# S5 matrices E built in their final layout from factors read with broadcast; q·B for eight groups at a time; adaLN pieces summed in one PSUM bank

## The chip, the core and the metric

The kernel runs on one core of a Trainium2 chip. Its metric is the time of one execution on the device, in microseconds (us), as the median of several runs. The core has five engines with a queue each, in which instructions run in order: TensorE (PE, with weight loads shown as PEld), VectorE (DVE), ScalarE (ACT), GpSimd (POOL) and SyncE (SP, which only issues transfers). They wait for each other through semaphores. Transfers issued by SP, ACT and POOL share 16 DMA engines.

## The reference, cut to what matters

One inference step of a two-layer backbone for 128 context tokens and 256 latent tokens (384 columns), width 1024. Each layer is a half-weighted SwiGLU, a mixer, a half-weighted SwiGLU; every sub-layer is modulated by adaLN vectors and followed by a layer norm. The mixer of layer 0 is a bidirectional S5 state-space layer:

```
x <- LayerNorm(ALPHA * x + w * gate * sublayer(x * (1 + scale) + shift))
(shift, scale, gate) = SiLU(cond) @ ada_w + ada_b            # per layer and sub-layer

abar = exp(dt * a)                                           # complex, per direction, group (64), state (64)
q    = (abar - 1) / a
bb   = q * b                                                 # complex, b: (group, state, 16)
s[t] = abar * s[t-1] + bb @ u[t]                             # forward, and backward in t
y    = Re(c @ s) + d_skip * u
```

The kernel runs the scan in blocks of eight tokens. For that it makes, from the parameters alone, three tables: E (what eight inputs add to a block's state: bb times powers of abar, one 128x128 matrix for each group and for the real and imaginary part), G (what a state gives to eight outputs: c times powers of abar) and the taps (the products of bb and G, for outputs from inputs inside a block).

## The kernel before, in words

Six sub-layers run one after the other: `ffn(0)`, `s5(1)`, `ffn(2)`, `ffn(3)`, `lru(4)`, `ffn(5)`. A float32 product is made of three TensorE products of rounded parts (`mm3`, lines 264 to 266): each weight tile of 1024 columns is fetched by SP into one of seven buffers `raw`, ACT makes `hi` from it (line 253) and DVE the rest `lo` (line 256); a step of `mm3` takes `hi` twice and `lo` once. I call the three matmuls of one `mm3` a step.

`ffn(0)` has 22 up-projection tiles, in splits of 8, 7 and 7, each split followed by a down loop over the eight output tiles m: up 0 (16 steps of `mm3` for each f), down 0 (64 steps), up 1 (112), down 1 (56), up 2 (112), down 2 (56). After every second k of an up tile, and three times in each m of down 0 and down 1, it calls `side()` from `beside(125, 42, 9)`. That is a slot, 124 up to the end of up 2. A slot either does one `ada_fill` (line 144: four matmuls of one half piece of `ada_w`, two trace instructions each; 42 of them, spread over 125 slots) or one step of the generator `s5_tables`. What is left of the generator at the end of up 2 is run through in `gen_done`, ahead of down 2. The order on PE is as written in the program; that of the other engines in `ffn(0)` is made by the scheduler, with the generator's instructions put some way ahead of their place (`high_priority`).

The generator first works out powers and q on DVE (steps up to line 684). Then, for each of 16 chunks `ch` of four groups, in five steps: `store_e` turns the four groups' E, eight PE transposes (line 731), two ACT copies into `s5eo` (732), and a store from the POOL queue to `etd` (734); `build_e(ch + 1)` loads 128 KB of b and c, negates c_re on DVE into `ncr` (692), makes bb by six DVE products and sums of 128x64 (lines 645 to 650, called through `cmul`), and E by six of 128x512; `taps` makes 16 small matmuls from bb and G (742), two ACT copies and two DVE additions, and a store to `kd`; `build_g(ch + 1)` makes the real part of G on DVE (716 to 718, 128x640) and the imaginary part on POOL (720 to 722), and stores it to `gd` from the POOL queue. E has one buffer, G two. `ada_w` loads go through the POOL queue too (line 127).

`ada_fill` sums the two halves of a piece in one PSUM bank; ACT copies the first piece of a group (151), DVE adds each further piece (153); `ada_flush` turns the sum with two matmuls (193).

`s5(1)` reads E, the taps and G back from memory. In its outputs part six more half pieces of `ada_w` run on PE between the products of tiles m (`ADAS = 4, 2`, after m = 2 and m = 3).

Of the kernel before, what the change touches and what calls it, by code (L numbers as in the profile page):

```python
# [23 lines left out]
Q = 8  # L24
# [10 lines left out]
ADAS = 4, 2  # L35
# [10 lines left out]
def backbone(ctx, tc, a, o):  # L46
# [60 lines left out]
    ada_acc = [None, None, 0]  # L107
# [22 lines left out]
    def ada_fill(n=1, load=True, bank=psaux, flush=True):  # L130


        for _ in range(n):
# [4 lines left out]
            if kh == 0:  # L138
                if flush:
                    ada_flush(bank)  # L140
                ada_acc[0] = bank()
            acc = ada_acc[0]
            for q in range(4):
                PE.matmul(acc[32 * q:32 * q + 32, :256], cond[:, kh * 4 + q, 6 - 2 * j:38 - 2 * j], w[:, q, :],  # L144
                          start=kh == 0, stop=kh == 1, tile_position=(0, 32 * q))
            if load:
                ada_load()
            if kh == 1:
                if j == 0:
# [4 lines left out]
                if j == len(group) - 1:  # L154
                    ada_pend.append((l, s, group, ada_acc[1]))
# [400 lines left out]
    kd = dram.tile([2048, 240], F32, name="kd")  # L556
    td = dram.tile([128, 64, 128], F32, name="td")
# [26 lines left out]
    def s5_tables(gp_):  # L584
# [49 lines left out]
        pw = gp_.tile([128, 2, 9, 64], F32, name="s5pw", tag="gch", bufs=2)  # L634
# [41 lines left out]
        pe = gp_.tile([128, 2, 8, 64], F32, name="s5pe")  # L676
# [10 lines left out]
        def build_e(ch):  # L687
            g0 = ch * 4
            bc = gp_.tile([128, 4, 64], F32, name="s5bc", tag="bc", bufs=2)
            nc.sync.dma_start(bc, a["s5bc"][ch])  # L690
            ncr = gp_.tile([128, 64], F32, name="s5ncr", tag="ncr")
            V.tensor_scalar(ncr, bc[:, 2, :], -1.0, None, op0=OP.mult)
            bb = gp_.tile([128, 2, 80], F32, name="s5bb", tag="bb", bufs=2)
            G.memset(bb[:, :, 64:80], 0.0)

            qv = lambda t: vw(t, g0, [[1, 4], [0, 16]])
            bv = lambda ri: vw(bc, ri * 64, [[16, 4], [1, 16]])
            ov = lambda ri: vw(bb, ri * 80, [[16, 4], [1, 16]])
            cmul(ov(0), ov(1), qv(sn), qv(cs), bv(0), bv(1), [[16, 4], [1, 16]])

            E = gp_.tile([128, 4, 2, 128], F32, name="s5E", tag="ech")
            pv = lambda ri: vw(pe, ri * 512 + g0, [[1, 4], [64, 8], [0, 16]])
            bv = lambda ri: vw(bb, ri * 80, [[16, 4], [0, 8], [1, 16]])
            ov = lambda ri: vw(E, ri * 128, [[256, 4], [16, 8], [1, 16]])
            cmul(ov(0), ov(1), pv(0), pv(1), bv(0), bv(1), [[128, 4], [16, 8], [1, 16]])
            return bc, ncr, bb, E

        def build_g(ch, bc, ncr):

            g0 = ch * 4  # L710
# [15 lines left out]
        def store_e(ch, E):  # L726
            eo = gp_.tile([128, 1024], F32, name="s5eo", tag="eo")
            for j in range(2):
                pt = psum()
                for b in range(4):  # L730
                    PE.transpose(pt[:, b * 128:b * 128 + 128], E[:, j * 2 + b // 2, b % 2, :], ident)
# [22 lines left out]
        for _ in range(9):  # L754
            yield
# [670 lines left out]
```

## Time and profile before

| | us |
|---|---|
| median of 3 runs | 1634.89 (1634.05 to 1637.48) |
| profiled execution, its own time | 1631.38 |
| span in that profile, first to last instruction | 1629.6 |
| PE busy, DVE busy, ACT busy, POOL busy | 1546.1, 1278.5, 709.4, 336.5 |
| mean granted TensorE clock, as a share of full | 0.974 |

All times further down are of that one profiled execution, counted from the span's start. A matmul's busy time is modelled and matmuls overlap, so two that follow each other start closer together than either lasts; the starts in the timeline tell PE's pace. Likewise a DVE instruction's record begins a little before the one ahead of it ends. The name in front of the arrow is the tile that is written.

### The profile page before, as it was taken

How to read it: one execution, taken by the hardware profiler on the slowest of the kernel's cores; microseconds unless marked ns; L12 is line 12 of the kernel's file. 1: busy time of each engine (PE TensorE's matmuls, PEld its weight loads, DVE VectorE, ACT ScalarE, POOL GpSimd, SP SyncE). 2: the span in 40 equal slices, each digit the busy share in tenths (PEclk: the TensorE clock that was granted, in tenths of full speed). 3: DMA queues.
4: the chain of work that ended last, by engine and by line, in shares of the span. 5: the costliest groups of instructions: out<-in, count | busy, mean ns of one | idle time of the engine just before them, and what ended most of it. 6: DMA issues, size and time to landing. Idle time of an engine off the chain costs nothing.

```text
span 1629.6 us, 25853 instructions
## 1 busy us (share of the span) xinstructions
PE 1546.1 (95%) x9554; PEld 1474.6 (90%) x9554; DVE 1278.5 (78%) x2750; ACT 709.4 (44%) x1157; POOL 336.5 (21%) x524
## 2 busy tenths in 40 slices
PE   7989999999988999999999999999989599999996
PEld 5877887889988999999999999999978599999995
DVE  4999999977796569979777998977797889644445
ACT  4423332335655366333345632334569366323332
POOL 0155445423380013000002300000165322000001
PEclk9989999999999999999999999999999799999997
DMA  9766776877878533667556356755513243544321
GB/s 352 260 215 224 232 244 237 259 244 275 129 272 257 201 133 118 230 202 243 173 171 208 117 188 214 243 193 160 193 64 118 76 157 123 160 153 139 100 77 39
DMA packets 108543, 301.19 MB, mean 185 GB/s; under 512 B 28384, under 2 KB 40160, under 8 KB 108160
## 3 DMA queue, kind: packets, MB, share of 16 engines
q1 hardware_dynamic: 85792, 249.62, 46.3%
q0 software_dynamic: 13152, 46.70, 8.7%
q10 hardware_dynamic: 9472, 3.21, 1.4%
q8 instruction: 75, 1.23, 0.3%
q14 instruction: 52, 0.43, 0.1%
HBM read 275.89 MB, written 27.80 MB: 186 GB/s over the span
## 4 chain that ended last, share of the span: by engine, by line
PE 70%; DVE 20%; DMA 3%; issue 3%; ACT 3%; POOL 1%; SPq 0%; ACTq 0%; DVEq 0%; POOLq 0%
PE mm L264 22%; PE mm L266 22%; PE mm L265 22%; DVE lo L256 2%; DVE hl L317 1%; PE aux L144 1%; DMA adaw<-in_ada_w 1%; DVE s5sb L881 1%; DVE w L878 1%; DVE w L460 1%; ACT w L322 1%; DVE lxc L1090 1%; PE mm L917 1%; DVE s5sb L880 1%; DVE w L879 1%
## 5 line engine op out<-in xcount | busy, mean ns | idle before, releaser
L264 PE MATMUL mm<-hh,hi 128*128 128x384 f32 (+1 forms) x1568 | 542.1, 346 | 14.5 <-DVE hh L1143 7.3
L265 PE MATMUL mm<-hl,hi 128*128 128x384 f32 (+1 forms) x1568 | 535.7, 342 | 10.2 <-DVE hl L317 10.1
L266 PE MATMUL mm<-hh,lo 128*128 128x384 f32 (+1 forms) x1568 | 535.4, 341 | 5.0 <-DVE lo L256 5.0
L253 ACT ACTIVATE hi<-raw 128x1024 fp32r<-128x1024 f32 (+1 forms) x332 | 323.2, 976 | 495.7 <-PE mm L265 467.1
L256 DVE TENSOR_TENSOR lo<-raw,hi 128x1024 fp32r<-128x1024 f32 (+1 forms) x344 | 393.6, 1148 | 164.4 <-ACT hi L253 154.1
L264 PEld LDWEIGHTS mm<-hh,hi 128*128 128x128 f32 x1568 | 298.7, 191 | 32.9 <-issue 15.7
L265 PEld LDWEIGHTS mm<-hl,hi 128*128 128x128 f32 x1568 | 299.0, 191 | 13.3 <-DVE hl L317 12.7
L266 PEld LDWEIGHTS mm<-hh,lo 128*128 128x128 f32 x1568 | 298.6, 190 | 7.0 <-DVE lo L256 7.0
L264 PE MATMUL mm<-zh,hi 128*128 128x384 f32 x704 | 240.5, 342 | 2.0 <-ACT zh L479 2.0
L265 PE MATMUL mm<-zl,hi 128*128 128x384 f32 x704 | 237.5, 337 | 1.8 <-DVE zl L480 1.6
L266 PE MATMUL mm<-zh,lo 128*128 128x384 f32 x704 | 237.0, 337 | 0.0
L264 PEld LDWEIGHTS mm<-zh,hi 128*128 128x128 f32 x704 | 132.9, 189 | 9.6 <-issue 6.3
L179 DVE SCALAR_TENSOR_TENSOR dump<-raw,cb 128x512 bf16<-128x512 f32 x160 | 109.9, 687 | 39.7 <-DMA raw<-in_ada_t 39.2
L265 PEld LDWEIGHTS mm<-zl,hi 128*128 128x128 f32 x704 | 133.1, 189 | 2.6 <-DVE zl L480 2.6
L266 PEld LDWEIGHTS mm<-zh,lo 128*128 128x128 f32 x704 | 133.2, 189 | 0.0
L479 ACT ACTIVATE zh<-w 128x384 fp32r<-128x384 f32 x88 | 46.1, 525 | 160.5 <-DVE w L487 154.1
L179 DVE SCALAR_TENSOR_TENSOR raw<-raw,cb 128x512 f32<-128x512 f32 x160 | 110.1, 688 | 2.6
L395 POOL TENSOR_TENSOR t<-mv 128x3 f32<-128x3 f32 x5 | 4.0, 799 | 446.0 <-ACT mv L394 446.0
L264 PE MATMUL mm<-ph,hi 128*128 128x388 f32 x224 | 77.4, 346 | 0.0
L265 PE MATMUL mm<-pl,hi 128*128 128x388 f32 x224 | 76.6, 342 | 0.0
L266 PE MATMUL mm<-ph,lo 128*128 128x388 f32 x224 | 76.3, 341 | 0.0
L545 DVE SCALAR_TENSOR_TENSOR r<-mm,gate,r 128x128 f32<-128x128 f32 (+1 forms) x144 | 53.2, 410 | 20.5 <-PE mm L266 20.5
(356 smaller groups left out, 1983.1 us busy)
## 6 DMA issues: line engine op xcount, KB each, us to landing
raw<-in_up SPq DMA_DIRECT2D x176, 512.0 KB, 4.4
raw<-in_ada_t SPq DMA_DIRECT2D x80, 512.0 KB, 4.2
raw<-in_down SPq DMA_DIRECT2D x56, 512.0 KB, 3.9
adaw<-in_ada_w POOLq DMA_DIRECT2D x42, 512.0 KB, 5.3
adaw<-in_ada_w SPq DMA_DIRECT2D x22, 512.0 KB, 7.9
raw<-in_down SPq DMA_DIRECT2D x48, 192.0 KB, 2.4
gd<-s5G POOLq DMA_DIRECT2D x16, 512.0 KB, 4.8
etd<-s5eo POOLq DMA_DIRECT2D x16, 512.0 KB, 5.5
```

The lines of the kernel that those rows point to most:

```text
L144: PE.matmul(acc[32 * q:32 * q + 32, :256], cond[:, kh * 4 + q, 6 - 2 * j:38 - 2 * j], w[:, q, :], start=kh == 0, stop=kh == 1, tile_positi ...
L179: V.scalar_tensor_tensor(out, wq, 1.0, cb[:, g, q * 512:q * 512 + 512], op0=OP.mult, op1=OP.mult, accum_out=part[:, t, g, q:q + 1])
L253: S.activation(hi[:, :n], raw[:, :n], AF.Copy)
L256: V.tensor_tensor(lo[:, :n], raw[:, :n], hi[:, :n], op=OP.subtract)
L264: PE.matmul(ps, hi[:, c:c + 128], xh, start=start, stop=False)
L265: PE.matmul(ps, hi[:, c:c + 128], xl, start=False, stop=False)
L266: PE.matmul(ps, lo[:, c:c + 128], xh, start=False, stop=stop)
L317: V.tensor_tensor(hl[:, k, :n], src, hh[:, k, :n], op=OP.subtract)
L322: S.activation(h[:, c0:c1], r[:, k, c0:c1], AF.Identity, bias=bs[:, k, g:g + 1], scale=gs[:, k, g:g + 1])
L460: V.scalar_tensor_tensor(t[:, c0:c1], self.ms[:, c0:c1], gw[:, g:g + 1], t[:, c0:c1], op0=OP.mult, op1=OP.add)
L479: S.activation(zh, z, AF.Copy)
L545: V.scalar_tensor_tensor(r[:, m, c0:c1], ps[:, c0:c1], gate[:, m, g:g + 1], r[:, m, c0:c1], op0=OP.mult, op1=OP.add)
```

## The change

In the generator:

- E is no longer built by state rows and turned. The factors are turned once: `pq` (q times the powers, six DVE instructions of 128x512) goes through eight PE transposes and is stored to a memory tensor `ptd`. For each chunk SP then reads `pt` (512 KB, every row of `ptd` to 16 partitions) and `bt` (256 KB, b in a new host layout, to eight groups of partitions), one chunk ahead and into two buffers each; six DVE instructions of 128x512 make E from them in the layout in which it is stored, and the store to `etd` goes out of E itself from the POOL queue. E keeps one buffer (tag `ech`, shared with the tables `pe` and `rows`).
- bb is made for eight groups (two chunks) at once, six DVE instructions of 128x128. `ncr` is made on POOL. b and c are loaded for two chunks at a time. G (tag `gch`) has one buffer instead of two.
- A chunk takes four steps of the generator instead of five.

In the adaLN pieces: all half pieces of a group are summed in one PSUM bank, which is copied once by ACT; DVE adds only where a group is closed early. `beside(125, 42, 9)` becomes `beside(125, 40, 9)` and `ADAS` becomes `4, 4`: two half pieces move from `ffn(0)` to `s5(1)`, where a load of `ada_w` follows the first four.

```
-ADAS = 4, 2
+ADAS = 4, 4
...
+            begin = acc is None
+            if begin:
+                acc = ada_acc[0] = bank()
+            done = kh == 1 and j == len(group) - 1
+            end = done or close and x == n - 1
             for q in range(4):
                 PE.matmul(acc[32 * q:32 * q + 32, :256], cond[:, kh * 4 + q, 6 - 2 * j:38 - 2 * j], w[:, q, :],
-                          start=kh == 0, stop=kh == 1, tile_position=(0, 32 * q))
+                          start=begin, stop=end, tile_position=(0, 32 * q))
...
-            if kh == 1:
-                if j == 0:
+            if end:
+                if ada_acc[1] is None:
...
-        pw = gp_.tile([128, 2, 9, 64], F32, name="s5pw", tag="gch", bufs=2)
+        pw = gp_.tile([128, 2, 9, 64], F32, name="s5pw", tag="gch")
...
+        def scaled(b):
...
+            cmul(ov(0), ov(1), qv(sn), qv(cs), bv(0), bv(1), [[16, 8], [1, 16]])
...
-            G.tensor_tensor(ov(1), cv(ncr, 0), pv(1), op=OP.mult)
-            G.tensor_tensor(p, cv(bc, 3), pv(0), op=OP.mult)
+            ncr = z
+            G.tensor_scalar(ncr, two["s5c"][ch // 2][:, 0, ch % 2 * 64:ch % 2 * 64 + 64], -1.0, None, op0=OP.mult)
+            G.tensor_tensor(ov(1), vw(ncr, 0, [[16, 4], [0, 10], [1, 16]]), pv(1), op=OP.mult)
+            G.tensor_tensor(p, cv(1), pv(0), op=OP.mult)
...
-                for b in range(4):
-                    PE.transpose(pt[:, b * 128:b * 128 + 128], E[:, j * 2 + b // 2, b % 2, :], ident)
-                S.activation(eo[:, j * 512:j * 512 + 512], pt, AF.Copy)
-                yield
-            nc.gpsimd.dma_start(etd[ch], eo)
...
+        cmul(pv(pq, 0), pv(pq, 1), pv(pe, 0), pv(pe, 1), qv(sn), qv(cs), [[64, 8], [1, 64]])
+        scaled(0)
+        Gt = build_g(0)
+        for _ in range(10):
+            yield
...
+        def load_e(ch):
+
+            pt = gp_.tile([128, 1024], F32, name="s5pt", tag="pt", bufs=2)
+            nc.sync.dma_start(pt, bass.AP(ptd.tensor, ptd.offset + ch * 1024, [[16384, 8], [0, 16], [1, 1024]]))
+            bt = gp_.tile([128, 512], F32, name="s5bt", tag="bt", bufs=2)
+            nc.sync.dma_start(bt, bass.AP(a["s5bt"].tensor, a["s5bt"].offset + ch * 8192, [[0, 8], [512, 16], [1, 512]]))
+            return pt, bt
+
+        def build_e(ch, pt, bt):
+
+            E = gp_.tile([128, 4, 2, 128], F32, name="s5E", tag="ech")
...
+            cmul(pv(E, 0), pv(E, 1), pv(pt, 0), pv(pt, 1), bv(0), bv(1), [[128, 4], [64, 2], [1, 64]])
+            nc.gpsimd.dma_start(etd[ch], E.rearrange("p g r c -> p (g r c)"))
...
         for ch in range(16):
-            yield from store_e(ch, cur[3])
-            nxt = build_e(ch + 1) if ch < 15 else None
+            taps(ch, two["bb"], Gt)
             yield
-            taps(ch, cur[2], Gt)
+            if ch < 15:
+                fac.append(load_e(ch + 1))
+            if ch % 2 and ch < 15:
+                scaled(ch // 2 + 1)
             yield
-            if nxt:
-                Gt = build_g(ch + 1, *nxt[:2])
-            cur = nxt
+            build_e(ch, *fac[ch])
+            yield
+            if ch < 15:
+                Gt = build_g(ch + 1)
...
-                        ada_load(6, nc.sync)
+                        ada_load(7, nc.sync)
...
-                                    ada_fill(ADAS[m - 2], False, psum, False)
+                                    ada_fill(ADAS[m - 2], False, psum, False, True)
+                                    if m == 2:
+                                        ada_load(4, nc.sync)
...
-        norm = ffn(0, (8, 7, 7), None, beside(125, 42, 9), gen_done, first)
+        norm = ffn(0, (8, 7, 7), None, beside(125, 40, 9), gen_done, first)
```

How this stands in the engines' queues: on PE, before, the end of up 2 holds the last E's eight transposes and the last taps (`mm<-s5G,s5bb`), directly ahead of down 2, whose first step is the one with `zh`:

```order
L266 MATMUL mm<-hh,lo 128x384
L731 MATMUL mm<-ident,s5E 128x128 x8
L742 MATMUL mm<-s5G,s5bb 32x128 x16
L144 MATMUL aux<-adaw,cond 32x256 x4
L264 MATMUL mm<-zh,hi 128x384
```

In the changed kernel (its line numbers are 6 to 34 higher; 270 to 272 are the three of a step) the last taps stand in the middle of up 2:

```order
L272 MATMUL mm<-hh,lo 128x384
L776 MATMUL mm<-s5G,s5bb 32x128 x16
L270 MATMUL mm<-hh,hi 128x384
L271 MATMUL mm<-hl,hi 128x384
L272 MATMUL mm<-hh,lo 128x384
```

No transposes stand there any more, and behind the last taps there are still 64 steps and six half pieces to the end of up 2.

On DVE, before, part of one chunk in up 1, from the end of a G to the first products of the next E (`s5bb` is bb, `s5tp` holds products):

```order
L718 TENSOR_TENSOR s5G<-s5tp 128x4x160
L645 TENSOR_TENSOR s5tp<-s5t_209,s5bc 128x64
L748 TENSOR_TENSOR s5ks<-s5ks,mm 128x16
L646 TENSOR_TENSOR s5tp<-s5t_210,s5bc 128x64
L749 SCALAR_TENSOR_TENSOR s5ks<-s5mask,s5dsk,s5ks 128x16
L647 TENSOR_TENSOR s5bb<-s5tp 128x64
L692 TENSOR_SCALAR s5ncr<-s5bc 128x64
L648 TENSOR_TENSOR s5tp<-s5t_209,s5bc 128x64
L649 TENSOR_TENSOR s5tp<-s5t_210,s5bc 128x64
L650 TENSOR_TENSOR s5bb<-s5tp 128x64
L645 TENSOR_TENSOR s5tp<-s5pe,s5bb 128x512
L646 TENSOR_TENSOR s5tp<-s5pe,s5bb 128x512
```

In the changed kernel, a chunk in up 1 without a new bb, from G to the end of E (`s5pt`, `s5bt` are the broadcast factors):

```order
L722 TENSOR_TENSOR s5G<-s5tp 128x4x160
L262 TENSOR_TENSOR lo<-raw,hi 128x1024
L652 TENSOR_TENSOR s5tp<-s5pt,s5bt 128x512
L653 TENSOR_TENSOR s5tp<-s5pt,s5bt 128x512
L782 TENSOR_TENSOR s5ks<-s5ks,mm 128x16
L654 TENSOR_TENSOR s5E<-s5tp 128x4x128
L783 SCALAR_TENSOR_TENSOR s5ks<-s5mask,s5dsk,s5ks 128x16
L655 TENSOR_TENSOR s5tp<-s5pt,s5bt 128x512
L656 TENSOR_TENSOR s5tp<-s5pt,s5bt 128x512
L657 TENSOR_TENSOR s5E<-s5tp 128x4x128
```

The six instructions of E have kept their size; those of bb are gone from this chunk and stand, twice as wide, in the next. Counted up to the last G write, DVE's queue holds 41 `lo` after the start of the power table instead of 51, and 12 evacuations of an up tile instead of 17.

## Rows read from the trace of the kernel before

**Rows 1.** The page's first part: busy us (share of the span), instructions.

```profile
PE 1546.1 (95%) x9554; PEld 1474.6 (90%) x9554; DVE 1278.5 (78%) x2750; ACT 709.4 (44%) x1157; POOL 336.5 (21%) x524
```

**Rows 2.** Windows: busy of PE, PEld, DVE, ACT, POOL; clock, DMA share, GB/s.

```profile
109.00:164.00 55.00, 49.86 (x398) 42.02 (x397) 54.19 (x89) 16.01 (x27) 28.83 (x30) 0.91 0.63 206
164.00:240.00 76.00, 76.00 (x597) 68.18 (x599) 73.31 (x118) 25.79 (x44) 34.40 (x40) 1.00 0.75 237
240.00:284.00 44.00, 39.98 (x342) 32.29 (x343) 42.70 (x71) 13.39 (x22) 21.87 (x25) 0.99 0.73 251
284.00:358.00 74.00, 74.00 (x606) 66.11 (x604) 65.58 (x111) 25.50 (x44) 28.79 (x36) 0.98 0.75 244
...
68.00:354.00 286.00, 274.88 (x2108) 239.62 (x2115) 275.28 (x475) 90.69 (x148) 129.10 (x146) 0.97 0.70 230
```

**Rows 3.** Timeline of PE in up 0: start us, us, what, count.

```profile
103.45 0.60 PE L731 MATMUL mm<-ident,s5E 128*128 128x128 f32 x4
...
104.07 0.34 PE L265 MATMUL mm<-hl,hi 128*128 128x384 f32 x1
104.24 0.34 PE L266 MATMUL mm<-hh,lo 128*128 128x384 f32 x1
```

**Rows 4.** Groups by line on PE, 68 to 354: count | busy, mean ns | idle before.

```profile
L144 PE MATMUL aux<-adaw,cond 128*32 128x256 f32 x304 | 25.2, 404 | 0.0
L731 PE MATMUL mm<-ident,s5E 128*128 128x128 f32 x120 | 20.3, 289 | 5.5 <-DVE s5E L650 4.7 <-DVE s5E L647 0.8
```

**Rows 5.** Single lines, whole trace: ns min/median/max, first and last start us.

```profile
L718 DVE TENSOR_TENSOR s5G<-s5tp x16: 812/824/1961, 97.4 to 353.5; 128x640 f32<-128x640 f32 x16
...
L731 PE MATMUL mm<-ident,s5E x128: 270/272/421, 103.4 to 357.3; 128*128 128x128 f32 x128
```

**Rows 6.** Groups by line and shape on DVE, 68 to 354.

```profile
L647 DVE TENSOR_TENSOR s5E<-s5tp 128x512 f32<-128x512 f32 x16 | 13.5, 844 | 4.0 <-PE mm L731 3.6
...
L153 DVE TENSOR_TENSOR adae<-adae,aux 128x256 f32<-128x256 f32 x15 | 6.2, 411 | 1.1 <-PE aux L144 1.1
...
L692 DVE TENSOR_SCALAR s5ncr<-s5bc 128x64 f32<-128x64 f32 x15 | 5.3, 356 | 0.4 <-DMA s5bc<-in_s5bc 0.4
...
L645 DVE TENSOR_TENSOR s5tp<-s5pw 128x128 f32<-128x128 f32 x1 | 0.3, 283 | 0.0
```

**Rows 7.** Timeline of DVE in down 0: start us, us, what.

```profile
132.50 1.21 DVE L256 TENSOR_TENSOR lo<-raw,hi 128x1024 fp32r<-128x1024 f32 x1
133.63 0.22 DVE L645 TENSOR_TENSOR s5tp<-s5t,s5bc 128x64 f32<-128x64 f32 x1
133.77 0.21 DVE L646 TENSOR_TENSOR s5tp<-s5t,s5bc 128x64 f32<-128x64 f32 x1
...
134.93 0.69 DVE L645 TENSOR_TENSOR s5tp<-s5pe,s5bb 128x512 f32<-128x512 f32 x1
135.54 2.06 DVE L646 TENSOR_TENSOR s5tp<-s5pe,s5bb 128x512 f32<-128x512 f32 x1
```

**Rows 8.** Timeline of POOL at the same place.

```profile
135.38 1.67 POOL L722 TENSOR_TENSOR s5G<-s5G,s5tq 128x640 f32<-128x640 f32 x1
```

**Rows 9.** Groups by line on POOL, 68 to 354.

```profile
L722 POOL TENSOR_TENSOR s5G<-s5G,s5tq 128x640 f32<-128x640 f32 x16 | 28.5, 1780 | 0.7
L720 POOL TENSOR_TENSOR s5G<-s5ncr,s5pg 128x640 f32<-128x640 f32 x16 | 25.2, 1576 | 6.0 <-PE mm L742 4.3 <-DVE s5pg L682 1.6
L721 POOL TENSOR_TENSOR s5tq<-s5bc,s5pg 128x640 f32<-128x640 f32 x16 | 24.3, 1518 | 5.4 <-DVE s5pg L682 4.2 <-DMA s5bc<-in_s5bc 0.4
...
L531 POOL TENSOR_SCALAR gate<-mod 128x16 f32<-128x16 f32 x1 | 0.4, 393 | 0.2 <-DVE s5ncr L692 0.2
```

**Rows 10.** DMA issues, 40 to 340: KB each, median us to landing.

```profile
etd<-s5eo POOLq DMA_DIRECT2D x14, 512.0 KB, 5.5
```

**Rows 11.** Timeline of PE in the outputs part of s5(1), with idle before.

```profile
502.03 6.87 PE L917 MATMUL mm<-al,raw 128*128 128x98 f32 x32 [3.94 <-DVE al L893]
...
522.30 3.78 PE L917 MATMUL aux<-al,raw 128*128 128x98 f32 x32 [1.29 <-ACT s5Y L921]
```

More of the change, by code (lines that the diff above doesn't have):

```diff
@@ L106, in backbone @@
     ada_done = set()
-    ada_acc = [None, None, 0]
+    ada_acc = [None, None]
     ada_pend = []
@@ L128, in ada_load, with ada_fill @@
             ada_loaded.append((c, w, extra))
-    def ada_fill(n=1, load=True, bank=psaux, flush=True):
-        for _ in range(n):
+    def ada_fill(n=1, load=True, bank=psaux, flush=True, close=False):
+        for x in range(n):
             if not ada_loaded:
@@ L153, in ada_fill @@
                     V.tensor_tensor(ada_acc[1], ada_acc[1], acc[:, :256], op=OP.add)
-                if j == len(group) - 1:
-                    ada_pend.append((l, s, group, ada_acc[1]))
+                ada_acc[0] = None
+            if done:
+                ada_pend.append((l, s, group, ada_acc[1]))
+                ada_acc[1] = None
     def vec_pool():
@@ L708, in build_g, with load2 @@
-        def build_g(ch, bc, ncr):
-            g0 = ch * 4
-            Gt = gp_.tile([128, 4, 2, 160], F32, name="s5G", tag="gch", bufs=2)
+        two = {"s5b": [], "s5c": []}
+        def load2(n, b):
+            two[n].append(gp_.tile([128, 2, 128], F32, name=n, tag=n, bufs=2))
+            nc.sync.dma_start(two[n][b], a[n][b])
+        def scaled(b):
+            bt = two["s5b"][b]
+            bb = gp_.tile([128, 2, 144], F32, name="s5bb", tag="bb")
+            G.memset(bb[:, :, 128:144], 0.0)
+            qv = lambda t: vw(t, b * 8, [[1, 8], [0, 16]])
+            bv = lambda ri: vw(bt, ri * 128, [[16, 8], [1, 16]])
+            ov = lambda ri: vw(bb, ri * 144, [[16, 8], [1, 16]])
+            cmul(ov(0), ov(1), qv(sn), qv(cs), bv(0), bv(1), [[16, 8], [1, 16]])
+            two["bb"] = bb
@@ L724, in build_g @@
             return Gt
[L726 to L729, printed above, removed]
[L730 to L734 removed]
+        for b in range(2):
+            load2("s5b", b)
+            load2("s5c", b)
+        pq = gp_.tile([128, 2, 8, 64], F32, name="s5pq", tag="pt", bufs=2)
+        pv = lambda t, ri: vw(t, ri * 512, [[64, 8], [1, 64]])
+        qv = lambda t: vw(t, 0, [[0, 8], [1, 64]])
+        cmul(pv(pq, 0), pv(pq, 1), pv(pe, 0), pv(pe, 1), qv(sn), qv(cs), [[64, 8], [1, 64]])
[3 more added lines that the diff above has]
+            yield
+        rows = gp_.tile([128, 2, 4, 128], F32, name="s5rows", tag="ech")
+        for ri in range(2):
+            ps = psum()
+            for b in range(4):
+                PE.transpose(ps[:, b * 128:b * 128 + 128], pq[:, ri, 2 * b:2 * b + 2, :].rearrange("p s g -> p (s g)"), ident)
+            S.activation(rows[:, ri].rearrange("p b c -> p (b c)"), ps, AF.Copy)
+            nc.gpsimd.dma_start(ptd.rearrange("(b s) g r p -> r (s g) b p", s=2)[ri], rows[:, ri])
+        yield
[7 more added lines that the diff above has]
+            E = gp_.tile([128, 4, 2, 128], F32, name="s5E", tag="ech")
+            pv = lambda t, ri: vw(t, ri * 128, [[256, 4], [64, 2], [1, 64]])
+            bv = lambda ri: vw(bt, ri * 64, [[128, 4], [0, 2], [1, 64]])
+            cmul(pv(E, 0), pv(E, 1), pv(pt, 0), pv(pt, 1), bv(0), bv(1), [[128, 4], [64, 2], [1, 64]])
+            nc.gpsimd.dma_start(etd[ch], E.rearrange("p g r c -> p (g r c)"))
         def taps(ch, bb, Gt):
@@ L750, in taps @@
             nc.gpsimd.dma_start(kd[ch * 128:ch * 128 + 128], ks)
-        cur = build_e(0)
-        Gt = build_g(0, *cur[:2])
-        for _ in range(9):
+        for _ in range(3):
             yield
+        fac = [load_e(0)]
         for ch in range(16):
-            yield from store_e(ch, cur[3])
-            nxt = build_e(ch + 1) if ch < 15 else None
+            taps(ch, two["bb"], Gt)
             yield
-            taps(ch, cur[2], Gt)
+            if ch < 15:
+                fac.append(load_e(ch + 1))
+            if ch % 2 and ch < 15:
+                scaled(ch // 2 + 1)
             yield
-            if nxt:
-                Gt = build_g(ch + 1, *nxt[:2])
-            cur = nxt
+            build_e(ch, *fac[ch])
+            yield
+            if ch < 15:
+                Gt = build_g(ch + 1)
+            if ch % 2 and ch < 13:
+                load2("s5b", ch // 2 + 2)
+                load2("s5c", ch // 2 + 2)
             yield
```

45 lines of the change are left out of this document (16 added, 29 removed).

## The prediction

> **What bounds the kernel now.** I read the page first, then windows cut at the stages of `ffn(0)`, then single groups. The page has PE busy for 95% of the span [rows 1], so only work that PE does, or waits for, can move the time. All that is changed lies between 68 us, where the generator's tables begin, and the end of up 2, but for six half pieces in `s5(1)`. There one must look at PE and DVE together. A matmul of a step starts 0.17 to 0.18 us after the one before (104.07 to 104.24, [rows 3]), so a step of three takes 0.525. By that down 0 needs 64 x 0.525 = 33.6 us, and took 55; up 1 112 x 0.525 = 58.8, and took 76; down 1 29.4, and took 44; up 2 58.8, and took 74 [rows 2]. DVE was busy for 54.2, 73.3, 42.7 and 65.6 us of these, and for 275.3 of the 286 us from 68 to 354 [rows 2]. In the down loops DVE is clearly the later one. In the up loops both are close to full.
>
> DVE's time is not all its own. In down 0 two products of E of the same size follow each other. The first lets the second start 0.61 us later; the second lasts 2.06 us [rows 7]. POOL's last step of a G ran from 135.38 to 137.05, just then [rows 8]. So I read DVE's long instructions as waits for POOL, and POOL's three instructions of a chunk as a toll on DVE that does not depend on which DVE instruction it hits. They take 28.5 + 25.2 + 24.3 = 78.0 us in this stretch [rows 9]. Mean durations of DVE's small instructions hold this toll and must not be counted as a saving when the instruction goes; the distance between starts, where POOL is quiet, is the price: 0.14 us for 128x64, 0.61 for 128x512, 1.13 for a `lo` of 1024 [rows 7].
>
> **PE's part.** Four transposes and one matmul of a step lie between 103.45 and 104.07, so four transposes cost 0.62 - 0.175 = 0.45 us [rows 3]. 128 were done, 8 stay: 30 fours, 13.5 us off PE. Two half pieces leave `ffn(0)`: 38 of them took 25.2 us [rows 4], 0.66 each, 1.3 off. PE also waited 5.5 us for E ahead of transposes [rows 4]. All of that, 20.3 us, is a gain only if PE is what ends last.
>
> **DVE's part, counted up to the last G.** PE can't do the last taps before the last G is there, and its order is fixed. Before, that G's write starts at 353.5 [rows 5] and the taps end up 2. In the changed order they stand 64 steps and six half pieces ahead of the end of up 2 (four generator steps to a chunk instead of five). So the question is when DVE reaches the last G.
> - Removed: 96 instructions of bb at 0.14 (13.4 us), 15 `ncr` at 0.14 or less (2.1), 15 additions of half pieces at 0.411 less an overlap of 0.08 (5.0) [rows 6, 7].
> - Added: 48 of 128x128 at 0.283 less 0.07 (10.1) [rows 6], six for `pq` at 0.61 (3.7).
> - E itself: six of 128x512 for a chunk as before; nothing is saved. Net so far -6.7 us.
> - Now behind the last G: the last E (6 x 0.61 = 3.7), ten `lo` (10 x 1.13 = 11.3), and five evacuations of two 128x384 instructions each, which I put between the 0.21 of 128 and the 0.61 of 512 columns, at 0.47 (4.7). Together -19.7 us.
> - `ncr` on POOL: 16 instructions; the nearest row is a POOL instruction of 128x16 with 0.39 us [rows 9]. As toll on DVE that is between 0 and 6.3 us; I take 3.
>
> DVE's busy time to the last G is then 275.3 - 6.7 - 19.7 + 3 = 251.9 us.
>
> A rule speaks against this move: the Trainium skill, "SBUF — State Buffer", section "Who interferes with whom", says that the port pair shared by DVE and GpSimd is an exclusive lock. The trace agrees with it, 2.06 against 0.69 us [rows 7, 8]. By it the 16 negations would cost DVE their full 6.3 us and the sum would come out 3.3 us higher; by the start distances alone, with no toll, 3 us lower.
>
> **DVE's idle time.** Before it was 286 - 275.3 = 10.7 us. Of that 3.6 us were waits for PE to read E and 1.1 for a half piece [rows 6]; both go. 6.0 remain. New: E has one buffer, and the next E may be written only when the store of the last one has landed, 5.5 us after its issue [rows 10], which must also get through POOL's queue. Between, DVE has a G (three at about 0.75), mostly one `lo` and two products of E, some 4.6 us of its own and up to 4.9 more of toll (78.0 / 16). In the chunks with bb there is more. So the wait is between nothing and about 1.4 us in half the chunks, 0 to 11 us with some delay in POOL's queue; I take 2, near the low end, since at DVE's pace of some 15 us for a chunk the store has time. The first E must also wait for the turned factors to be stored and read back: 0 to 5.5 us, I take 2. Later reads of the factors are issued a chunk ahead. Idle 10 us in all.
>
> **The sum.** Last G at 68 + 251.9 + 10 = 330. Behind it PE has 64 x 0.525 + 6 x 0.66 = 37.6 us to the end of up 2: 367.5. Before, the last transposes start at 357.3 [rows 5], and 0.6 of taps and a half piece (0.66) follow: 358.5. So up 2 ends 9 us later. DVE finishes the last E in the meantime; down 2 and what follows is as before. PE's 20 us don't show, because PE waits in the stages where it could gain. In `s5(1)` two more half pieces cost 1.3 us, behind which stood a wait of 1.29 us for ACT [rows 11]: between 0 and 1.3, I take 0.5. The last half piece is loaded behind the fourth; 3.9 us of idle and 6.9 us of work [rows 11] cover a landing of 5.5; without that cover PE would wait for the rest of it. More DMA (16 x 768 KB instead of 16 x 128) is 10.5 MB in some 260 us, 40 GB/s on top of 230 at a share of 0.70 [rows 2]: about 0.82, no bound; ACT's 30 copies fewer lie beside PE's work. In all +9.5 us on the profiled execution's 1631.4: 1640.9. The median stands 3.5 us above that execution, so 1644.4, rounded 1644.5.
>
> **Rivals.**
> - *DVE gets by with less toll.* POOL's instructions may fall more often into DVE's idle time or beside work that they don't block. Each us of toll less is a us earlier. From 9.5 us, an eighth of the 78.0, there is no loss; with a fifth less (15.6) it is 6 us faster, 1629. For it speaks that a DVE that waits for stores is not hit; against it that DVE has so little idle time. 0.16.
> - *PE is the bound.* Then all of PE's 20.3 us less the 0.5 in `s5(1)` is gained: 1615. The last taps would stand at 358.5 - 20.3 - 37.6 = 300.6, so DVE would have to reach the last G in 232 us instead of 262. Nothing in the trace [rows 2, 7] lets me find 30 us. 0.06.
> - *It comes out even*, within 0.2% or 3.3 us, about what a measurement of this kernel can tell from no change: toll and idle time a little lower than taken. 0.14.
> - *The single E buffer decides.* If POOL's queue, which waits in order for `ada_w` buffers, landings of G and the taps, holds the store back by some 2 us for each E, the store ends after DVE's own work in most chunks, and 16 chunks lose about 1 us each beyond what I took: 1660. It decides from the point where issue and landing together exceed DVE's 5 to 9 us between two E. 0.12.
> - That the change does not do what it says I leave out: the order shows it.
>
> The forecast, slower by 4 to 16 us because the chunks stand closer together on PE than DVE can build them, has the remaining 0.52.
>
> **How the numbers follow.** Slower: 0.52 + 0.12 = 0.64; same 0.14; faster 0.16 + 0.06 = 0.22. The range takes in the low-toll case down to 1627 and half of the case of the single buffer, up to 1656; about 2 in 10 are left out.
>
> **What would show it.** In the changed profile: the last taps at about 330, the end of up 2 near 367; DVE 94% busy or more from 68 to 330; the chunks' growth visible most in down 1, where DVE has most chunks for the fewest steps, with PE idle there for G or `lo` and its clock lower; DVE's E instructions still 0.6 to 0.7 us when POOL is quiet; waits of the E write for a store of 0 to 2 us. I am wrong if the last taps come before 320, if DVE shows idle time of tens of us there while PE waits for nothing, or if the loss lies outside `ffn(0)`.

## The result, and the profile after

The changed kernel takes 1684.99 us (1683.72 to 1692.59), the kernel before, on the same chip, 1635.68 us (1634.05 to 1637.48): 1.0311 of its time, 95% interval 1.0278 to 1.0344. It is slower, as I forecast, but by 51 us and not by 9.5, and outside the range. The page's first part, beside [rows 1]:

```profile
PE 1543.3 (92%) x9434; PEld 1473.1 (88%) x9434; DVE 1268.2 (75%) x2671; ACT 691.4 (41%) x1127; POOL 347.8 (21%) x532
```

PE and DVE are both less busy than before, in a longer span (1681.9 against 1629.6 us): it is waiting that was added. Windows of the changed kernel answer to [rows 2]: first the stretch from the power table to the last taps, then down 0, up 1, down 1 and up 2. Columns as there.

```profile
68.00:367.00 299.00, 236.83 (x1771) 206.88 (x1769) 246.63 (x378) 63.11 (x104) 142.84 (x150) 0.87 0.72 235
104.90:168.00 63.10, 45.53 (x362) 39.54 (x360) 47.85 (x72) 10.94 (x18) 27.89 (x31) 0.84 0.69 229
168.00:261.00 93.00, 76.48 (x572) 67.39 (x571) 81.71 (x107) 21.71 (x37) 44.51 (x47) 0.87 0.77 244
261.00:328.00 67.00, 45.04 (x360) 37.57 (x358) 48.31 (x80) 10.95 (x19) 36.04 (x37) 0.82 0.72 240
328.00:406.00 78.00, 71.87 (x519) 63.88 (x517) 54.42 (x72) 21.79 (x36) 31.92 (x39) 0.96 0.80 278
```

Down 0 takes 63 us (55 before), up 1 93 (76), down 1 67 (44), up 2 78 (74). Up 2 ends at 406.0 us instead of 358.7: 47.3 of the 52.3 us of span. DVE, which I had full up to the last taps, worked for 246.6 of 299 us. In the three slow stages the granted clock was 0.82 to 0.87, and 0.91 to 1.00 before. What PE waited for from 60 to 500 us (us in total, times, longest), and the taps' line:

```profile
PE mm L776 <- DVE s5G L722: 60.1, 11, 11.4
...
PE mm L776 <- POOL s5G L728: 1.0, 1, 1.0
```

```profile
L776 PE MATMUL mm<-s5G,s5bb x512: 266/414/420, 109.5 to 367.6; 64*32 64x128 f32 x171
```

PE waits for one thing, the next G, ahead of the taps, 61 us in all. From the first to the last taps are 258 us for 15 chunks, 17.2 us each; I had counted on 15. What DVE and POOL waited for in the same stretch:

```profile
DVE s5E L654 <- DMA etd<-s5E: 29.1, 8, 9.9
DVE lo L262 <- ACT hi L259: 16.8, 12, 3.7
DVE s5tp L652 <- DMA s5pt<-ptd: 7.9, 1, 7.9
```

```profile
POOL s5G L726 <- DMA gd<-s5G: 60.9, 12, 9.0
...
POOL gd L729 <- DVE s5G L722: 24.1, 11, 6.3
```

POOL waits 61 us for the store of the last G to land before it may write the next: a wait that [rows 9] don't have, where G has two buffers. One turn of this on POOL's timeline (start us, us, what):

```profile
186.74 1.33 POOL L726 TENSOR_TENSOR s5G<-s5t,s5pg 128x640 f32<-128x640 f32 x1 [7.32 <-DMA gd<-s5G]
188.16 2.42 POOL L728 TENSOR_TENSOR s5G<-s5G,s5tq 128x640 f32<-128x640 f32 x1
190.56 0.94 POOL L725 TENSOR_SCALAR s5t<-s5c 128x64 f32<-128x64 f32 x1
191.47 1.33 POOL L727 TENSOR_TENSOR s5tq<-s5c,s5pg 128x640 f32<-128x640 f32 x1
192.75 0.60 POOL L767 DMA_DIRECT2D etd<-s5E  x1
193.35 0.55 POOL L127 DMA_DIRECT2D adaw<-in_ada_w  x1
193.87 0.93 POOL L729 DMA_DIRECT2D gd<-s5G  x1
...
202.92 1.35 POOL L726 TENSOR_TENSOR s5G<-s5t,s5pg 128x640 f32<-128x640 f32 x1 [7.44 <-DMA gd<-s5G]
```

The turn closes on itself: 7.1 us from the first write of a G to the issue of its store, 9.1 from there to the first write of the next, 16.2 us. E's store (L767) stands inside it, behind POOL's wait and POOL's instructions of G: over the 16 chunks it is issued 0.3 to 11.0 us after E is done, 3.1 in the mean (ends of L657 on DVE against starts of L767). On DVE this shows as a wait of the first write of E, in down 1:

```profile
290.61 0.69 DVE L654 TENSOR_TENSOR s5E<-s5tp 128x512 f32<-128x512 f32 x1 [9.87 <-DMA etd<-s5E]
...
295.51 2.02 DVE L657 TENSOR_TENSOR s5E<-s5tp 128x512 f32<-128x512 f32 x1
```

```profile
283.74 0.54 POOL L767 DMA_DIRECT2D etd<-s5E  x1
284.26 0.91 POOL L729 DMA_DIRECT2D gd<-s5G  x1
292.72 0.56 POOL L784 DMA_DIRECT2D kd<-s5ks  x1 [7.54 <-DVE s5ks L783]
...
295.16 1.82 POOL L728 TENSOR_TENSOR s5G<-s5G,s5tq 128x640 f32<-128x640 f32 x1
```

DVE's wait begins at 280.7, three us before E's store is even issued (283.74), and lasts until 290.61; in DVE's queue the taps' additions, the next `lo` and the next G stand behind it, and POOL then waits for those additions. PE gets its G from DVE last: here POOL's half is done at 296.98, DVE's at 301.38, and the taps start at 301.52 (DVE's and PE's timeline):

```profile
299.74 1.64 DVE L722 TENSOR_TENSOR s5G<-s5tp 128x640 f32<-128x640 f32 x1
```

```profile
301.52 1.11 PE L776 MATMUL mm<-s5G,s5bb 64*32 64x128 f32 x32 [11.19 <-DVE s5G L722]
```

In all eleven waits for DVE's G the taps start within 0.2 us of its end, and in ten of them POOL's half had been done for 3 to 14 us. So POOL's late turn reaches PE through E's store and DVE, not by its own half of G.

Stores land later than before, too: median from issue to landing of the page's and the trace's DMA groups, against 5.5 us for E before [rows 10]. After:

```profile
gd<-s5G POOLq DMA_DIRECT2D x16, 512.0 KB, 7.6
...
etd<-s5E POOLq DMA_DIRECT2D x16, 512.0 KB, 7.1
```

Before, on the page:

```profile
gd<-s5G POOLq DMA_DIRECT2D x16, 512.0 KB, 4.8
```

### The profile page after: what moved, and what is told of

It reads as the page before. It is cut to its first block, busy times and chain, and to the rows that moved or that the text cites. A ratio compares the mean times of both kernels' runs of the same rounds, so it can differ in the third digit from the quotient of the medians.

```text
span 1681.9 us, 25536 instructions
## 1 busy us (share of the span) xinstructions
PE 1543.3 (92%) x9434; PEld 1473.1 (88%) x9434; DVE 1268.2 (75%) x2671; ACT 691.4 (41%) x1127; POOL 347.8 (21%) x532
## 4 chain that ended last, share of the span: by engine, by line
PE 61%; DVE 13%; ACT 2%; POOL 1%; issue 1%; DMA 0%; ACTq 0%; DVEq 0%
PE mm L270 19%; PE mm L271 19%; PE mm L272 19%; DVE hl L323 1%; DVE w L466 1%; DVE s5sb L920 1%; DVE w L917 1%; DVE lo L262 1%; ACT w L328 1%; DVE lxc L1131 1%; PE mm L956 1%; DVE s5sb L919 1%; DVE w L918 1%; PE mm L900 1%; DVE r L436 1%
## 5 line engine op out<-in xcount | busy, mean ns | idle before, releaser
L776 PE MATMUL mm<-s5G,s5bb 64*32 64x128 f32 x512 | 14.7, 350 | 61.0 <-DVE s5G L722 60.1
```

## The experiments

Ratios are to the kernel before on the same chip. "Single" and "double" tell of the buffers of G and E.

| run | edit to the changed kernel (or as said) | ratio (95%) |
|---|---|---|
| the change | both single, four steps a chunk | 1.0311 (1.0278 to 1.0344) |
| g_two | G double, c, b, bt in one buffer | 1.0328 (1.0307 to 1.0348) |
| g_two_b | G double, b, bt in one buffer | 1.0211 (1.0191 to 1.0230) |
| e_two | E double, c, b, bt in one buffer | 1.0262 (1.0240 to 1.0284) |
| e_inplace | E double (in place) | 1.0194 (1.0168 to 1.0220) |
| eg_two | both double (E in place), b in one buffer | 1.0123 (1.0101 to 1.0145) |
| five_only | both single, fifth step in ten chunks | 1.0229 (1.0194 to 1.0265) |
| eg_five | both double, fifth step in ten chunks | 1.0008 (0.9991 to 1.0024) |
| eg_early | eg_five, factors turned earlier | 0.9980 (0.9965 to 0.9996) |
| no_reload | factors loaded for two chunks only | 1.0212 (1.0191 to 1.0233) |
| before_g_one | kernel before, G single | 0.9985 (0.9974 to 0.9996) |
| before_ada | kernel before, pieces in one bank, 40 and 4, 4 | 1.0024 (1.0012 to 1.0036) |

### Which buffer

My theory A was that G's single buffer closes the loop above; B, that E's does; C, that neither matters. g_two:

```
-        Gt = gp_.tile([128, 4, 2, 160], F32, name="s5G", tag="gch")
+        Gt = gp_.tile([128, 4, 2, 160], F32, name="s5G", tag="gch", bufs=2)
```

> The changed kernel with G in two buffers again; room for it comes from smaller things (one buffer for bt, b and c; the taps' tile laid over dead tables). E stays in one buffer. Theory A (the single G buffer sets the chunks' distance: store issue 0.9, landing 7.6, then POOL's two G instructions 3.3, two more 2.3, queued issues 1.5, about 15.6 of the 17.2 us from taps to taps, and E's store waits behind it in POOL's queue): the 61 us that PE waits for G fall under 15, the last taps come before 335, time 1640 to 1655. Theory B (the single E buffer holds DVE up, 29 us, and G is late for that): 1672 to 1685, DVE's wait for the E store stays above 20 us. Theory C (neither buffer; DVE and POOL need this long in the changed order): 1678 to 1690.

e_two has `bufs=2` on `ech` instead.

> The changed kernel with E in two buffers, G in one; the same smaller things give the room. Theory A: DVE's wait for the E store goes (29 to under 3 us), PE's wait for G stays above 45, time 1672 to 1685. Theory B: 1640 to 1655. Theory C: 1678 to 1690.

eg_two has G so, and E without a tile of its own: it is written over `pt` (`er`, `ei`, `br`, `bi` are views of `pt` and `bt`):

```
-            E = gp_.tile([128, 4, 2, 128], F32, name="s5E", tag="ech")
...
-            cmul(pv(E, 0), pv(E, 1), pv(pt, 0), pv(pt, 1), bv(0), bv(1), ...)
...
+            V.tensor_tensor(p[0], ei, bi, op=OP.mult)
+            V.tensor_tensor(p[1], er, bi, op=OP.mult)
+            V.tensor_tensor(er, er, br, op=OP.mult)
+            V.tensor_tensor(ei, ei, br, op=OP.mult)
+            V.tensor_tensor(er, er, p[0], op=OP.subtract)
+            V.tensor_tensor(ei, ei, p[1], op=OP.add)
```

> The changed kernel with G in two buffers and E written in place over its broadcast factor, which has two buffers already (so E has two as well and its own 4 KB a partition go; b in one buffer). Theories A and B: the time that I predicted from DVE's work alone, 1638 to 1650, last taps near 330, DVE idle some 10 us from 68 to 330. Theory C: above 1670.

> The kernel before with one G buffer instead of two, nothing else. There G lands in 4.8 us and a chunk has five steps, 15 to 18 us. Theory A: issue 0.9, landing 4.8, POOL's G 4.7 and queued issues 1.5 make about 12 us, under the distance of the chunks in the up loops and near that of the down loops: 0 to 12 us slower, 1635 to 1647, most of it in down 1. Theories B and C: within 3 us of before.

g_two was no faster than the change (1688.0 us) and so seemed to refute A. It doesn't: with c in one buffer POOL stood for c instead, in every second chunk, a wait of my own making (POOL's waits, g_two):

```profile
POOL s5t L727 <- DMA s5c<-in_s5c: 57.3, 7, 12.2
```

e_two has the same fault, 20 us of it. Hence the next two runs, without it: c stays double; e_inplace is eg_two with G single and b double.

> G in two buffers, E in one, with c kept in two buffers (in g_two POOL waited 57 us for c, so that run says nothing of G); the room comes from b and bt in one buffer and from two tiles laid over dead ones. If G's buffer is most of the loss: 1655 to 1662, the wait of DVE for E's store under 15 us. If E's single buffer is enough to hold the chunks at their distance: 1672 to 1690, that wait 20 us or more.

> The changed kernel with E written in place over its broadcast factor (two buffers), everything else kept, G in one buffer. It is the single E buffer taken away alone, without the smaller buffers of e_two, where POOL waited 20 us for c. If the two single buffers add up (E 8 us by e_two, the rest G): 1672 to 1680. If they hold each other up in POOL's queue, so that only both together bring much: PE's wait for G stays above 45 us and the time is 1665 to 1678. If E's buffer alone decides: 1650 to 1658.

Each buffer by itself takes some 16 to 19 us away (1.0311 to 1.0211 and 1.0194), both 31 (1.0123). So neither A nor B, as I had put them, was right: the two add up, nearly. None of the three times lay in a range that I had written down (g_two_b 1664.9 us, e_inplace 1664.1, eg_two 1654.6). PE's waits for G in g_two_b, e_inplace and eg_two, in this order:

```profile
PE mm L784 <- DVE s5G L725: 49.9, 9, 15.6
```

```profile
PE mm L781 <- DVE s5G L722: 37.9, 10, 11.8
PE mm L781 <- POOL s5G L728: 5.2, 4, 2.4
```

```profile
PE mm L782 <- DVE s5G L722: 39.8, 10, 15.6
```

With E double alone POOL still waited for G's landing, 40.9 us from 60 to 420 (60.9 in the change); with G double alone DVE still waited 9.4 us for E's store (29.1), which was now issued 0.5 us in the mean after E was done (3.1):

```profile
POOL s5G L726 <- DMA gd<-s5G: 40.9, 11, 5.1
```

```profile
DVE s5E L658 <- DMA etd<-s5E: 9.4, 4, 6.0
```

In eg_two these waits are gone but for 4.7 us of POOL's, and DVE is nearly full: its window from 68 to the last taps, and the taps' line.

```profile
68.00:340.00 272.00, 231.26 (x1802) 201.84 (x1801) 254.43 (x383) 64.97 (x107) 158.88 (x153) 0.92 0.81 265
```

```profile
L782 PE MATMUL mm<-s5G,s5bb x512: 266/293/420, 109.6 to 339.7; 64*32 64x128 f32 x171
```

254.4 us busy and 17.6 idle up to the last taps at 340: this is nearer to the kernel that I had forecast (251.9, 10, 330), with PE waiting for G still.

In the kernel before, the same single G buffer costs nothing (0.9985), where theory A had 0 to 12 us. There POOL, from 60 to 420 us, waits mostly for the taps that read G, and only twice for its store:

```profile
POOL s5G L720 <- PE mm L742: 35.8, 12, 5.5
...
POOL s5G L720 <- DMA gd<-s5G: 5.9, 2, 4.3
```

So it isn't the edit by itself: there the store has mostly landed by the time the taps have run. The programs' order fits this: before, a G is made four generator steps ahead of its taps and the next one follows a step behind them; in the change it is one step ahead and three behind. In the change G also lands later (a median of 7.6 us, 4.4 in before_g_one) and the chunks stand closer. Which of these made the edit costly I did not separate.

### Traffic

no_reload leaves out the loads of `pt` and `bt` after the second chunk (E's values are then those of the first two):

```
+            if ch > 1:
+                return fac[ch % 2]
             pt = gp_.tile([128, 1024], F32, name="s5pt", tag="pt", bufs=2)
```

> The changed kernel, where the factors pt and bt are loaded for the first two chunks only and these are used for all later E (the values of E are left out of the reference's; the same instructions run). It takes 14 x 768 KB of DMA out. If the longer landings of G and E (7.6 and 7.1 us instead of 4.8 and 5.5) come from this traffic, they fall to 5 to 6 us, and with them 1.5 to 2.5 us for each of 15 chunks on the chain of G's store: 1645 to 1665. If not, landings stay above 7 us and the time is 1678 to 1688.

1667.6 us, just above the range. Landings in no_reload:

```profile
gd<-s5G POOLq DMA_DIRECT2D x16, 512.0 KB, 6.1
etd<-s5E POOLq DMA_DIRECT2D x16, 512.0 KB, 4.6
```

With the added reads the stores land 1.5 and 2.5 us later, and with single buffers that costs 0.99% or 16 us, 1 us a chunk. I had written that a DMA share of 0.82 is "no bound". It came out at 0.72 from 68 to 367 us, and landings were longer all the same: a loop that waits for a landing needs no bound to be slowed.

### Cadence

eg_five and five_only put a fifth step into the first ten chunks, on eg_two and on the change:

```
             taps(ch, two["bb"], Gt)
-            yield
+            for _ in range(2 if ch < 10 else 1):
+                yield
```

> eg_two with a fifth step of the generator in each of the first ten chunks, so that the last taps stand at step 468 of 472 of the up and down loops instead of 408. Theory (chunks stand closer on PE than DVE builds them): PE waits for G under 15 us instead of 39.8, the last taps near 357, end of up 2 at 357 to 363 instead of 377, time 1634 to 1642. Rival (each chunk takes DVE and POOL 15 us wherever it stands, and lo that come between make it longer): last taps 365 to 375, 1645 to 1655.

> The changed kernel, both buffers single as in it, with the fifth step in the first ten chunks alone. Theory (two separate losses, buffers and cadence, that share the same waits of PE): the chunks then stand 30 steps apart, 16 us, and the chain of G's store takes 17, so that only the last chunks have to catch up: more than half of the 51 us goes, 1640 to 1660. Rival (the chain of stores sets the distance whatever stands on PE): the last taps stay at 365 or later but fall at the end of up 2, so up 2 ends near 370: 1645 to 1650. If the buffers were the whole loss: 1675 to 1690.

With both buffers double this takes 19 us away, all that was left (1.0123 to 1.0008); 1630.5 us, where I expected 1634 to 1642. PE's waits for G fell from 39.8 us, though not under 15:

```profile
PE mm L782 <- DVE s5G L722: 26.9, 5, 14.0
```

With single buffers it takes 13 (1.0311 to 1.0229), and the last taps come at 390 us, at the end of up 2:

```profile
L776 PE MATMUL mm<-s5G,s5bb x512: 266/293/420, 109.3 to 390.0; 64*32 64x128 f32 x171
```

That is 18.7 us a chunk: with single buffers this cadence does not get the kernel back. The median, 1671.0 us, lies between what I expected of the theory and of the buffers alone; the profiled execution took 1677.8.

### What the rest costs

eg_ada_back is eg_two with 42 half pieces in the first sub-layer and 4, 2 in `s5(1)`; before_ada is the kernel before with this part of the change alone.

> eg_two with 42 half pieces in the first sub-layer and 4 and 2 in s5(1) as before, and without the loads added there; the sum in one bank is kept. Theory: the outputs part of s5(1) takes 43.0 us again instead of 46.8, 1.3 us of PE's in the first sub-layer lie beside its waits for G: 3 to 5 us faster than eg_two, 1649.5 to 1652. Rival: the 3.7 us there come from other things (E and G read later): 1653 to 1656.

> The kernel before with the second part of the change alone: pieces summed in one bank, 40 half pieces in the first sub-layer, 4 and 4 in s5(1) with the load between. By my sum: 5.0 us of additions go from DVE, which bounds the first sub-layer, two half pieces from PE there, and s5(1) gains 0.5: 1626 to 1630. Rival (the outputs part of s5(1) takes 3.7 us more, as in the changed kernel): 1629 to 1634.

eg_ada_back: 1.0118 (1.0091 to 1.0144) beside 1.0123, no difference that these runs show. before_ada: 0.24% slower, 3.9 us; 1635.9 us where I expected 1626 to 1630. The five us of DVE additions that it saves are not gained; its taps stand 3 to 12 steps earlier in most chunks, and PE waits 7.8 us for E where [rows 4] have 5.5, and 5.6 for `zh` where it had been 2.0.

eg_early and eg_best turn the factors three steps earlier (`range(10)` to `range(7)`); eg_best also has the pieces as in eg_ada_back and no negation of c:

```
+        V.tensor_scalar(pg[:, 1], pg[:, 1], -1.0, None, op0=OP.mult)
...
-            V.tensor_tensor(ov(0), p[0], p[1], op=OP.subtract)
+            V.tensor_tensor(ov(0), p[0], p[1], op=OP.add)
...
-            G.tensor_scalar(ncr, two["s5c"][ch // 2][:, 0, ...], -1.0, None, op0=OP.mult)
-            G.tensor_tensor(ov(1), vw(ncr, ...), pv(1), op=OP.mult)
+            G.tensor_tensor(ov(1), cv(0), pv(1), op=OP.mult)
```

> eg_five with the turned factors three generator steps earlier on PE (seven steps after their products instead of ten), so that they are stored and read back before the first E wants them. Theory: DVE's 9.4 us of waiting for the first pt, behind which the second G stands, and PE's 14 us for that G are a part of the loss that I had priced at 2: 5 to 12 us faster than eg_five, 1619 to 1626. Rival: DVE catches up with such a hole later on, and what ends last is its work up to the last G anyway: within 2 us of eg_five, 1629 to 1633.

> eg_early with two more edits: the half pieces are 42 and 4, 2 again (the sum in one bank stays), and no c is negated any more: the imaginary powers are negated once (one DVE instruction of 128x640) and the real part of G adds where it subtracted. That takes POOL's 16 negations away, 0.82 us each by eg_two, 13.2 us in which DVE may be held up. Theory: 3 us from s5(1) and 3 to 10 from POOL's toll on DVE: 1608 to 1619. Rival (the toll falls into DVE's waits): 1617 to 1623.

eg_early (1629.1 us, as the rival had it) was 0.28% faster than eg_five by the two ratios, about the bound of what can be told; DVE still waited 9.9 us for the first `pt`, so it did not test that wait. eg_best came out slower, 1.0034 (1.0019 to 1.0048). Its last taps stand at the very end of up 2. There ACT's copy of them waits for the store of the taps before to land, since their tile `s5ks` has one buffer too, and `zh` stands behind that copy in ACT's queue. PE waits 9.6 us for it (the other 8.6 lie at the start of down 0); my words for eg_last below put this down to the last E. ACT's timeline and PE's waits in eg_best:

```profile
363.82 0.28 ACT L785 ACTIVATE s5ks<-mm 128x128 f32<-128x128 f32 x1 [11.63 <-DMA kd<-s5ks]
```

```profile
PE mm L270 <- ACT zh L485: 18.2, 2, 9.6
```

In the change ACT waits 19.9 us for the same store, in two pieces (5.4 before); PE does not wait for ACT there.

early_g_first puts the next G ahead of E and leaves the negations out, early_g_first_ncr keeps them, early_g_first_ada is the first with the pieces put back:

```
-            build_e(ch, *fac[ch])
-            yield
             if ch < 15:
                 Gt = build_g(ch + 1)
+            for _ in range(3 if ch == 0 else 1):
+                yield
+            build_e(ch, *fac[ch])
```

> In eg_early DVE still waited 9.9 us for the first pt, since the read of it lands 20 us after PE's turn, so that run did not test what the wait costs. Here each chunk makes the next G ahead of its E, so that the second G does not stand behind that wait; a fifth step in chunks 1 to 6 and two more ahead of the first E; no c is negated (imaginary powers negated once). Theory: PE's waits for G, 12 us in eg_early, go to under 5 and the 13 us of POOL's negations take some DVE time with them: 1616 to 1624. Rival (DVE's work up to the last G ends last whatever its holes): 1624 to 1631.

> early_g_first with POOL's negations of c kept: the difference of the two is what 16 small instructions on POOL cost DVE. My prediction took 3 us (0 to 6.3); by the 0.82 us that each lasts it is up to 13. Theory: 2 to 8 us slower than early_g_first. Rival: no difference over 2 us, since they run in POOL's waits.

> early_g_first with 42 half pieces in the first sub-layer and 4, 2 in s5(1), the group closed early there, and a fifth step in chunks 1 to 4 only, so that the last taps stand at the same step 456. Theory (the outputs part of s5(1) gets its 3 to 4 us back, two half pieces cost 1.3 on PE and a DVE addition more): 2 to 3 us faster than early_g_first. Rival: the first sub-layer gives it back, within 1 us.

The theory of the first fell, and its rival with it: 1640.9 us, 1.0051 (1.0032 to 1.0071), slower than eg_early. PE still waited 14.8 us for G (12.1 in eg_early), and 16.4 for `zh` and `w` (7.1 for `zh`). The second gave 1.0054 (1.0036 to 1.0071): in this kernel the 16 negations cost nothing that can be measured. Windows of the two, without and with them:

```profile
68.00:349.00 281.00, 255.11 (x1983) 222.94 (x1981) 258.93 (x390) 70.05 (x116) 132.00 (x140) 0.95 0.83 267
```

```profile
68.00:349.00 281.00, 254.15 (x1941) 221.67 (x1942) 260.19 (x389) 69.94 (x116) 143.55 (x154) 0.95 0.82 264
```

11.5 us of POOL's work more are 1.3 us of DVE's. The third gave 1.0023 (1.0009 to 1.0037), 0.28% faster than the first, with the last taps at the same step: here the pieces cost 4.6 us.

eg_last was to put all of this together, with the last taps at step 456, and eg_early ran again beside it.

> eg_early (both buffers double, E ahead of G, factors turned early) with the half pieces of before, 42 and 4, 2, and a fifth step in the first six chunks only, so that the last taps stand at step 456 and not 468: eg_best, whose last taps stood at 472, paid 9.6 us there for a zh behind the last E. Theory: eg_early less the 2.8 us by which early_g_first_ada beat early_g_first, 0.996 of before, 1622 to 1629. Rival (the chunks are closer by that much in the later part, and PE waits for G again): 1629 to 1636.

> eg_early once more, beside eg_last on the same chip: 0.997 to 0.9995 of before, and eg_last 1 to 5 us faster by the theory, or slower than it by the rival.

eg_last: 1.0018 (1.0003 to 1.0033), eg_early 0.9983 (0.9970 to 0.9995). The rival held: in eg_last, whose chunks stand closer in down 1, PE waited 15.5 us for G, and 11.3 in eg_early beside it. The best version that I found is eg_early: 54 us faster than the change, and 0.2% faster than the kernel before, at the edge of what can be told.

## Why the prediction was wrong

**What bounds the kernel.** Right. The loss is inside `ffn(0)` for nine tenths, DVE and PE together set it, and the distance behind the last taps came out as counted: 38.8 us from 367.2 to 406, forecast 37.6.

**DVE's part.** Right. I forecast 251.9 us of work up to the last G. The change has 246.6 us in its window, eg_two 254.4.

**POOL's toll.** The size was off, and it did not matter. I took 3 us for the negations. They take 12.6 us on POOL (group on POOL, 68 to 367):

```profile
L725 POOL TENSOR_SCALAR s5t<-s5c 128x64 f32<-128x64 f32 x16 | 12.6, 788 | 0.4 <-DVE s5pw L644 0.3
```

The pair early_g_first shows 1.3 us of it on DVE and nothing in the time; in the change itself, where DVE has more idle time, I did not test it. The Trainium skill, "SBUF — State Buffer", section "Who interferes with whom", calls the port pair that DVE and GpSimd share an exclusive lock, and single instructions agree with that (295.51: 2.02 us, beside POOL's from 295.16). That such locks add up to a toll of POOL's whole time was my own step, and the pair does not bear it out.

**DVE's idle time.** This is the step that failed. I forecast 10 us up to the last taps, and the window has 299 - 246.6 = 52.4. Its terms:

- E's single buffer, priced at 2 us (0 to 11), has 29.1 us of waits. I compared issue and landing with DVE's own work between two E, with a landing of 5.5. It was 7.1, and the store left 3.1 us late in the mean, since POOL's queue was held by G; with G double alone it left 0.5 us late, and the wait was 9.4.
- The first read of the turned factors, priced at 2 (0 to 5.5), has 7.9.
- G's single buffer, which the change names, has no term of its own; only the rival of the single E buffer counts landings of G among what POOL's queue waits for. The sum looks at DVE, where G's store shows 0.9 us in this stretch. It acts on POOL, 60.9 us, and from there on E's store, on DVE and on DVE's half of the next G. For POOL's half PE waits once, 1.0 us; in e_inplace, where the first write of E no longer waits for a store, four times, 5.2 us.

The other 14.5 us are small waits, for which I had kept 6.0.

By this the last taps come at 367 instead of 330, 37 us of the profiled execution's miss of 43 (1683.7 against 1640.9). Of the rest 1 lies behind the last taps and 5 in `s5(1)` and later: the first statistics product of PE in down 2 (the first matmuls of the layer norm) starts at 440.3 us, 393.4 before, 46.8 us later, and the last instruction ends 52.3 later. For the single E buffer I had a rival with the right mechanism, POOL's queue in order, and a chance of 0.12; its price of 1 us a chunk was half of what the store's wait alone came to (29.1 / 16 = 1.8).

**Four steps for a chunk.** I counted that PE would wait, and 9 us of loss by it. Where the buffers are out of the way (eg_two) the loss is 1.23%, 20 us. Its profiled span is 23.5 us longer than before's: the 9.5 forecast, 10 more since the last taps come at 340 and not at 330, with the first wait for `pt` (9.3 us, 2 counted) in it, and 4 later on. A fifth step gives all of it back. So the direction rested on a step that holds, and the size on one that was left out.

**s5(1).** Forecast 0.5 us. In the outputs part of the change (PE's timeline, beside [rows 11]):

```profile
543.12 1.93 PE L148 MATMUL mm<-adaw,cond 128*32 128x256 f32 x32
550.51 6.29 PE L956 MATMUL mm<-al,raw 128*128 128x98 f32 x32 [5.46 <-DVE al L932]
556.73 1.93 PE L148 MATMUL mm<-adaw,cond 128*32 128x256 f32 x32
...
572.13 5.41 PE L956 MATMUL aux<-al,raw 128*128 128x98 f32 x32 [2.58 <-ACT hi L259]
```

From the first products to the end of the last the part takes 46.7 us, 43.1 before. The second group of half pieces takes 0.9 us more, the wait for `al` 1.5 more, the last products 1.6 more (5.41 against 3.78 for the same 32) and the wait ahead of them 1.3 more; others take less. I had let a wait absorb the added work; the wait grew. The runs with the pieces put back don't agree on what this is worth: 4.6 us in one pair, nothing that shows in the other, and on the kernel before the whole part cost 3.9 us. It stays open.

**Chances.** All the rivals but one lay below the forecast. That one, POOL's queue holding back E's store, was right in kind, and the range took in only half of it, up to 1656.

## What to carry to other kernels

When a change takes a buffer away, write down the whole turn of that buffer, first write, issue, landing, next write, with every instruction that stands between them in the same queue, and compare it with the time that one turn may take; do it on the engine that writes, not on the one that looks busiest. A tile that is stored and not read again needs its second buffer for the landing alone, and the landing is to be taken with the traffic that the change adds. And the same edit can be free in one kernel and cost 12 to 16 us in the next: G's second buffer is worth 0.71 and 1.00% here (e_inplace to eg_two, the change to g_two_b), nothing in before_g_one.

## What was not expected of the hardware

- Stores of 512 KB from POOL's queue landed in a median of 4.8 us (G, before), 6.1 (no_reload) and 7.6 (the change). The Trainium skill, "DMA: Bandwidth & Descriptors", section "Anatomy of one DMA — SWDGE (gpsimd) path", has a fit of 2.0 us and 436 KB for each further us, by which 512 KB would take an estimated 3.2 us; no such store had a lower median than 4.3 in any run (G in before_ada).
- A POOL negation of 128x64 takes 0.79 us in the change, twice the 0.39 of a 128x16 one [rows 9].
- PE also ran slower in the stretches in which it waited. In down 1, where it was busy for 45.0 of 67 us, its window shows a granted clock of 0.82 (0.99 before, busy for 40.0 of 44 [rows 2]), and the median of the taps' small matmuls over the whole trace is 414 ns where 266 is the least; their line in eg_five and eg_early has 269. What this costs beside the waits themselves no run here separates.
